# Retention in chunks of 64 tokens on quarters of the PE array, with a second copy of the values

## The chip, the cores and the metric

The program runs on one core of a Trainium2 chip. Its engines are TensorE (PE in the profile, with its weight loads shown as PEld), VectorE (DVE), ScalarE (ACT), GpSimd (POOL) and SyncE (SP), which here issues most DMAs. Each engine works through a fixed list of instructions in order and waits at semaphores for the others. The metric is device time in microseconds for one execution, the median of several runs.

## The reference

The program is a two-layer trunk on 1024 tokens of width 1024, in float32. Layer 0 has two branches, a state-space branch with a GLU, and retention with 8 heads (keys and queries of 64, values of 128); layer 1 is a convolution module. The change touches only the retention, which the reference computes in chunks of 64 tokens:

```python
CHUNK = 64
def retention(q, k, v):
    q = rope(q, positions) * (RET_DK ** -0.5)
    k = rope(k, positions)
    log_g = jnp.log(1.0 - 2.0 ** (-5.0 - jnp.arange(RET_HEADS)))
    intra = jnp.exp(log_g[:, None, None] * jnp.abs(idx[:, None] - idx[None, :]))
    ...
    scores = jnp.einsum('bnihd,bnjhd->bnhij', qc, kc) * intra
    intra_out = jnp.einsum('bnhij,bnjhe->bnihe', scores, vc)
    k_dec = jnp.exp(log_g[None, :] * (CHUNK - 1 - idx)[:, None])
    kv = jnp.einsum('bnjhd,jh,bnjhe->bnhde', kc, k_dec, vc)
    def state_step(s, kv_n):
        return chunk_decay * s + kv_n, s
    _, s_prev = lax.scan(state_step, zeros, kv)
    cross = jnp.einsum('bnihd,ih,bnhde->bnihe', qc, q_dec, s_prev)
    out = intra_out + cross
    mu = jnp.mean(out, axis=-1); var = jnp.mean((out - mu) ** 2, axis=-1)
    return (out - mu) * lax.rsqrt(var + EPS)
```

## The kernel before

Everything lives in one class. The retention is a stage in the middle of layer 0: `retention` (L926) runs four pairs of heads. The two heads of a pair lie on partitions 0 to 63 and 64 to 127, so that one tile of 128 partitions holds the keys (`krot`) or the queries (`qrot`) of both. `ret_proj` projects keys and queries of a pair (the 512-wide products `mm_k` and `mm_q`, through the helper at L276 to L278) and rotates them. `ret_values` (before pair 0) makes the values of all heads by products and sums into the tiles `v`, with 128 tokens on the partitions and the block of tokens as a free index.

`ret_heads` (L1079) does one pair, in blocks of 128 tokens, that is two of the reference's chunks; a mask sets to zero what a query of the first chunk would take from a key of the second. Its steps, in the names of the profile:

- `ktp`, `kt`: the keys are transposed to tokens on partitions (8 products) and multiplied by a decay (DVE, L1090).
- `kv` (L1107): 14 products, per block and head, each on half of the array (128 tokens deep, 64 wide), into two PSUM banks, one for each half of the sequence (`hf`).
- `S` (L1115, L1117): DVE turns them into the states before each block, one after the other: a copy and 6 steps S[b+1] = g S[b] + kv[b]. These form a chain.
- `sp` (L1124): the scores, 16 products, each on half of the rows; a bank for each head and half. `sc` (L1130): the scores times the mask, 4 instructions of 128x512 on DVE.
- `ro`: for each half of the sequence, first the products of states and queries (L1154, half of the rows each, called cross below), then those of masked scores and values (L1159, the full array, called intra below), into a bank for each head.
- `st`, `mv`, `rs`, `on` (L1168 to L1174): mean and variance of each row on DVE, the square root on ACT (L552), the reciprocal on DVE (L553), the normalised rows on DVE. ACT also casts weights for layer 1 in this stage (`lh` from `lf`, L232, made by `weight_low`), and its list of instructions is in order.
- `rt` (L1182): the normalised rows are transposed back, 8 products for each half of the sequence; they wait for `on`. They are multiplied by the gate `grl` and stored.

All of these products are float32, and the profile counts two instructions for each: 14 products of `kv` are 28 matmul rows. A product with a moving side of 512 columns (`mm_...`, in a faster float32 form) is one row.

The order on each engine is no list in the source: a scheduler places the instructions by priority and by a simulated time for each, `issue_after` and `chained` add constraints, and tile pools add waits for free buffers. So the 512-wide products of the next pair's projections (`mm_q`, `mm_k`) and, in the last two pairs, of the GLU (`mm_glu`) stand between the retention products. PSUM has 8 banks: five for the tag "aux" (all of `kv`, `sp`, `ro`, `rt` and others) and three for `mm`.

## Time and profile before

| what | before |
|---|---|
| median of 3 runs | 1178.66 us (1176.93 to 1179.49) |
| span of the profiled execution, first to last instruction | 1173.9 us |
| PE busy in the span | 1161.3 us |
| DVE, ACT, POOL busy | 910.5, 545.1, 713.5 us |
| the profile's chain of work that ended last | 91% on PE |

The profile gives the span of the profiled execution and no other time for it. The median of the runs lies 4.8 us above that span. In the rows below, a timeline row has the start in us, the duration, the engine, the line, the operation, output and inputs, the shape of the array's part that is used (128*64 is 128 rows by 64 columns), the shape of the moving side and the count; at its end in brackets stands how long the engine was idle before it and who released it. "sp<-qrot,krot 64*128 64x128 f32 x18" is 18 matmul instructions on half of the rows.

### The profile page before, as it was taken

The page shows a single profiled execution, that of the slowest core. Times are in us where ns is not written, and L with a number is a line of the kernel's source. Part 1 is how long each engine was busy: PE and PEld are TensorE (multiplying, and loading weights), DVE is VectorE, ACT ScalarE, POOL GpSimd, SP SyncE. Part 2 cuts the span into 40 slices and gives each one's busy share as a digit, 9 for nine tenths or more (in the row PEclk, how much of TensorE's full clock was granted, in tenths as well). Part 3 has the DMA queues.
Part 4 walks back from the last instruction along what each step waited for, and adds up shares of the span by engine and source line. Part 5 has one row for each costly group of instructions (what it writes and reads, how often), then busy time and mean ns, then how long its engine had stood idle before and what let it go on. Part 6 is the DMA issues. An engine that isn't in the chain of part 4 may idle for free.

```text
span 1173.9 us, 17492 instructions
## 1 busy us (share of the span) xinstructions
PE 1161.3 (99%) x6150; PEld 965.5 (82%) x6150; DVE 910.5 (78%) x1507; ACT 545.1 (46%) x821; POOL 713.5 (61%) x507
## 2 busy tenths in 40 slices
...
GB/s 344 109 178 109 134 270 312 272 269 282 273 307 325 268 228 192 251 190 180 362 313 304 160 220 268 309 232 188 161 158 306 216 182 132 134 176 243 281 247 138
DMA packets 131192, 270.66 MB, mean 231 GB/s; under 512 B 12832, under 2 KB 41760, under 8 KB 130976
## 3 DMA queue, kind: packets, MB, share of 16 engines
...
q10 hardware_dynamic: 1152, 4.19, 0.9%
...
## 4 chain that ended last, share of the span: by engine, by line
PE 91%; DMA 4%; DVE 2%; SPq 1%; ACT 1%; POOL 1%; issue 1%; DVEq 0%; POOLq 0%; ACTq 0%
PE mm_g L277 8%; PE mm_g L278 8%; PE mm_g L276 7%; PE mm_w L278 4%; PE mm_w L277 4%; PE mm_w L276 4%; PE mm_a L278 2%; PE mm_b L277 2%; PE mm_a L276 2%; PE mm_b L278 2%; PE mm_a L277 2%; PE mm_b L276 2%; PE mm_u L278 2%; PE mm_oc L278 2%; PE mm_u L277 2%; PE mm_oc L277 2%
## 5 line engine op out<-in xcount | busy, mean ns | idle before, releaser
L1461 DVE SCALAR_TENSOR_TENSOR cv<-u,convw,cv 128x512 f32<-128x512 f32 x358 | 244.7, 750 | 5.0 <-ACT cv L1447 3.5
L1441 POOL TENSOR_TENSOR tp<-tp,tp 128x512 f32<-128x512 f32 x104 | 138.9, 1338 | 28.7 <-ACT tp L1440 23.4
L278 PE MATMUL mm_g<-xh,wl_g 128*128 128x512 f32 x256 | 100.8, 394 | 0.0
L277 PE MATMUL mm_g<-xl,wh_g 128*128 128x512 f32 x256 | 100.7, 394 | 0.0
L276 PE MATMUL mm_g<-xh,wh_g 128*128 128x512 f32 x256 | 100.5, 393 | 0.0
L1440 ACT ACTIVATE tp<-u,convw 128x512 f32<-128x512 f32 x104 | 69.6, 713 | 9.6 <-POOL tp L1441 9.4
L277 PEld LDWEIGHTS mm_g<-xl,wh_g 128*128 128x128 f32 x256 | 48.1, 188 | 11.2 <-issue 1.6
L278 PEld LDWEIGHTS mm_g<-xh,wl_g 128*128 128x128 f32 x256 | 48.0, 188 | 10.5
L276 PEld LDWEIGHTS mm_g<-xh,wh_g 128*128 128x128 f32 x256 | 48.1, 188 | 9.6
L278 PE MATMUL mm_oc<-zh,wl_woc 128*128 128x512 f32 (+1 forms) x152 | 54.5, 360 | 0.2 <-DMA wl_woc<-lo_woc 0.2
L276 PE MATMUL mm_oc<-zh,wh_woc 128*128 128x512 f32 (+1 forms) x152 | 54.3, 362 | 0.0
L277 PE MATMUL mm_oc<-zl,wh_woc 128*128 128x512 f32 (+1 forms) x152 | 54.0, 357 | 0.0
L276 PE MATMUL mm_glu<-yh,wh_glu 128*128 128x512 f32 x128 | 50.0, 392 | 1.3 <-ACT sg L1250 1.3
L277 PE MATMUL mm_u<-xl,wh_u 128*128 128x512 f32 x128 | 50.1, 391 | 1.0 <-DVE xl L390 0.9
L276 PE MATMUL mm_g<-h1h,wh_cg 128*128 128x512 f32 x128 | 50.3, 393 | 0.0
L276 PE MATMUL mm_a<-h1h,wh_ca 128*128 128x512 f32 x128 | 50.3, 393 | 0.0
L278 PE MATMUL mm_b<-h1h,wl_cb 128*128 128x512 f32 x128 | 50.3, 393 | 0.0
L232 ACT CAST lh<-lf 128x512 fp32r<-128x512 f32 x32 | 19.5, 618 | 65.9 <-DMA lf<-w_c 59.3
L278 PE MATMUL mm_a<-h1h,wl_ca 128*128 128x512 f32 x128 | 50.0, 391 | 0.0
L277 PE MATMUL mm_glu<-yl,wh_glu 128*128 128x512 f32 x128 | 50.0, 392 | 0.0
L278 PE MATMUL mm_g<-h1h,wl_cg 128*128 128x512 f32 x128 | 49.9, 390 | 0.0
L277 PE MATMUL mm_g<-h1l,wh_cg 128*128 128x512 f32 x128 | 49.9, 390 | 0.0
...
## 6 DMA issues: line engine op xcount, KB each, us to landing
...
```

Source lines behind the costliest of these rows:

```text
L232: self.nc.scalar.copy(hi[:], f[:])
L276: nc.tensor.matmul(ps, wh[:, kb, :], xh, start=start, stop=False)
L277: nc.tensor.matmul(ps, wh[:, kb, :], xl, start=False, stop=False)
L278: self.last_mm = nc.tensor.matmul(ps, wl[:, kb, :], xh, start=False, stop=stop)
L1440: nc.scalar.mul(sk[:], u[:, k:k + HALF], cw[:, nb, k:k + 1])
L1441: gp.tensor_tensor(s0[:], s0[:], sk[:], op=ALU.add)
L1461: v.scalar_tensor_tensor(dst[:], *tap, accs_[i][:], op0=ALU.mult, op1=ALU.add)
```

## The change

A block becomes a chunk of 64 tokens, as in the reference.

- All products of a pair run on quarters of the array (64 rows by 64 columns). `kv`: 30 instead of 14, in two banks by the parity of the chunk in its block. `sp`: 32 instead of 16, with 64 moving columns instead of 128, and both heads' scores in one bank, on its lower and upper partitions, instead of a bank each. Cross: 30 instead of 14. Intra: 32 on quarters instead of 16 on the full array.
- 15 states instead of 7: a copy and 14 steps on DVE. The masked scores take 2 DVE instructions instead of 4.
- The mask shrinks from 512 KB to 128 KB and the decay table from 256 KB to 4 KB; nothing of a score is set to zero any more.
- On a quarter, the rows that hold the scores of a head must also hold the values, so a chunk whose values lie in the other half of the partitions needs them moved. `crossed(pair)` makes the tile `vx`, the values of the pair with the two halves of each block exchanged, by 4 DMAs of 128 KB from SBUF to SBUF on SP's queue; it is called for pair 0 behind `ret_values`, and for the next pair behind `ret_heads`. There is one buffer for `vx`. `value(..., own=True)` picks it.

```diff
@@ -941,11 +941,11 @@
...
         nc.sync.dma_start(self.rk[:], A["rope_k"])
-        self.mask = r0.tile([P, NH, P], F32, name="retmask")
+        self.mask = r0.tile([P, 4, 64], F32, name="retmask")
         nc.sync.dma_start(self.mask[:], A["ret_mask"])
-        self.g128 = r0.tile([P, 4], F32, name="g128")
-        nc.sync.dma_start(self.g128[:], A["ret_g128"])
-        self.kdec = r0.tile([P, NH, 64], F32, name="kdec")
+        self.g64 = r0.tile([P, 4], F32, name="g64")
+        nc.sync.dma_start(self.g64[:], A["ret_g64"])
+        self.kdec = r0.tile([P, NH], F32, name="kdec")
         nc.sync.dma_start(self.kdec[:], A["ret_kdec"])
...
@@ -955,6 +955,7 @@
...
                     V = self.ret_values(self.pool("vp", 1, stack=vst))
+                self.crossed(0)
                 self.rp = self.pool("ret", 1, stack=st)
...
@@ -970,6 +971,8 @@
...
             self.ret_heads(pair, *cur, V, turned)
+            if pair < 3:
+                self.crossed(pair + 1)
     def ret_proj(self, pair):
...
@@ -1074,7 +1077,22 @@
...
                     self.y_pass(vp, cb)
-        return lambda p, b, hh: vt[p // 2][b // 4][:, b % 4, (2 * (p % 2) + hh) * P:(2 * (p % 2) + hh + 1) * P]
+        def value(p, c, hh, own=False):
+            d, h, b, i = p // 2, c // 8, c // 2 % 4, p % 2
+            if own and c % 2 != hh:
+                return self.vx[:, c // 2, :]
+            return vt[d][h][:, b, (2 * i + hh) * P:(2 * i + hh + 1) * P]
+        return value
+
+    def crossed(self, pair):
+
+        d, i = pair // 2, pair % 2
+        self.vx = self.r0.tile([P, 8, P], F32, name=f"vx{pair}", tag="vx", bufs=1)
+        for h in range(2):
+            for hh in range(2):
+                to, of = slice(64 * hh, 64 * hh + 64), slice(64 - 64 * hh, 128 - 64 * hh)
+                self.nc.sync.dma_start(self.vx[to, 4 * h:4 * h + 4, :],
+                                       self.vt[d][h][of, :, (2 * i + hh) * P:(2 * i + hh + 1) * P])
     def ret_heads(self, pair, K, Q, qadds, V, turned):
...
@@ -1086,51 +1104,43 @@
...
                 nc.tensor.transpose(ps[:, b * P:(b + 1) * P], K[:, t0:t0 + P], self.ident[:])
-            kd = self.kdec[:, 2 * pair:2 * pair + 2, :].rearrange("p h d -> p (h d)")
-            self.last_kt = v.tensor_tensor(kt[:, 4 * hf:4 * hf + 4, :], ps[:].rearrange("p (b d) -> p b d", b=4),
-                                           kd.unsqueeze(1).broadcast_to([P, 4, P]), op=ALU.mult)
+            kd = self.kdec[:, 2 * pair:2 * pair + 2].unsqueeze(1).unsqueeze(3).broadcast_to([P, 4, 2, 64])
+            self.last_kt = v.tensor_tensor(
+                kt[:, 4 * hf:4 * hf + 4, :].rearrange("p b (h d) -> p b h d", h=2),
+                ps[:].rearrange("p (b h d) -> p b h d", b=4, h=2), kd, op=ALU.mult)
         with self.tc.issue_after(self.last_kt.ins):
...
         turned()
-        S = rp.tile([P, 8, P], F32, name=f"S_{pair}", tag="S", bufs=1)
+        S = rp.tile([P, 15, P], F32, name=f"S_{pair}", tag="S", bufs=1)
+        half = lambda i: slice(64 * i, 64 * i + 64)
         for hf in range(2):
-            ps = self.bank(f"kv{hf}_{pair}")
-            for b4 in range(4):
-                b = 4 * hf + b4
-                if b == 7:
-                    continue
-                for hh in range(2):
-                    r = slice(64 * hh, 64 * hh + 64)
-                    nc.tensor.matmul(ps[r, b4 * P:(b4 + 1) * P], kt[:, b, r], V(pair, b, hh),
-                                     start=True, stop=True)
-            for b4 in range(4):
-                b = 4 * hf + b4
-                if b == 7:
-                    continue
-                kv = ps[:, b4 * P:(b4 + 1) * P]
-                if b == 0:
-                    v.tensor_copy(S[:, 1, :], kv)
+            kvs = [self.bank(f"kv{hf}{par}_{pair}") for par in range(2)]
+            cs = [c for c in range(8 * hf, 8 * hf + 8) if c < 15]
+            col = lambda c: slice(c // 2 % 4 * P, (c // 2 % 4 + 1) * P)
+            self.chained(nc.tensor.matmul(kvs[c % 2][half(hh), col(c)], kt[half(c % 2), c // 2, half(hh)],
+                                          V(pair, c, hh)[half(c % 2)], start=True, stop=True)
+                         for c in cs for hh in range(2))
+            for c in cs:
+                kv = kvs[c % 2][:, col(c)]
+                if c == 0:
+                    v.tensor_copy(S[:, 0, :], kv)
                 else:
-                    v.scalar_tensor_tensor(S[:, b + 1, :], S[:, b, :], self.g128[:, pair:pair + 1], kv,
+                    v.scalar_tensor_tensor(S[:, c, :], S[:, c - 1, :], self.g64[:, pair:pair + 1], kv,
                                            op0=ALU.mult, op1=ALU.add)
         self.masked = [None, None]
-        sc = [rp.tile([P, 8, P], F32, name=f"sc{hh}_{pair}", tag=f"sc{hh}", bufs=1) for hh in range(2)]
+        sc = rp.tile([P, 16, 64], F32, name=f"sc_{pair}", tag="sc", bufs=1)
         for hf in range(2):
-            sps = [self.bank(f"sp{hf}{hh}_{pair}") for hh in range(2)]
-            self.chained(nc.tensor.matmul(sps[hh][:, b4 * P:(b4 + 1) * P],
-                                          K[64 * hh:64 * hh + 64, (4 * hf + b4) * P:(4 * hf + b4 + 1) * P],
-                                          Q[64 * hh:64 * hh + 64, (4 * hf + b4) * P:(4 * hf + b4 + 1) * P],
+            sps = self.bank(f"sp{hf}_{pair}")[:].rearrange("p (c i) -> p c i", c=8)
+            tok = lambda c: slice(c * 64, (c + 1) * 64)
+            self.chained(nc.tensor.matmul(sps[half(hh), c % 8, :], K[half(hh), tok(c)], Q[half(hh), tok(c)],
                                           start=True, stop=True)
-                         for b4 in range(4) for hh in range(2))
-            for hh in range(2):
-                self.masked[hf] = v.tensor_tensor(
-                    sc[hh][:, 4 * hf:4 * hf + 4, :], sps[hh][:].rearrange("p (b i) -> p b i", b=4),
-                    self.mask[:, 2 * pair + hh, :].unsqueeze(1).broadcast_to([P, 4, P]), op=ALU.mult)
-
+                         for c in range(8 * hf, 8 * hf + 8) for hh in range(2))
+            self.masked[hf] = v.tensor_tensor(sc[:, 8 * hf:8 * hf + 8, :], sps,
+                                              self.mask[:, pair, :].unsqueeze(1).broadcast_to([P, 8, 64]), op=ALU.mult)
         if pair == 2:
...
@@ -1146,18 +1156,17 @@
...
             def products():
-                for b4 in range(4):
-                    b = 4 * hf + b4
+                cs = range(8 * hf, 8 * hf + 8)
+                out = lambda c, hh: pss[hh][half(c % 2), c // 2 % 4 * P:(c // 2 % 4 + 1) * P]
+                for c in cs:
                     for hh in range(2):
-                        r = slice(64 * hh, 64 * hh + 64)
-                        if b:
-                            yield nc.tensor.matmul(pss[hh][:, b4 * P:(b4 + 1) * P], Q[r, b * P:(b + 1) * P],
-                                                   S[r, b, :], start=b4 == (hf == 0), stop=False)
-                for hh in range(2):
-                    for b4 in range(4):
-                        b = 4 * hf + b4
-                        yield nc.tensor.matmul(pss[hh][:, b4 * P:(b4 + 1) * P], sc[hh][:, b, :],
-                                               V(pair, b, hh), start=False, stop=b4 == 3)
+                        if c:
+                            yield nc.tensor.matmul(out(c, hh), Q[half(hh), tok(c)], S[half(hh), c - 1, :],
+                                                   start=c in (2, 1, 8, 9), stop=False)
+                for c in cs:
+                    for hh in range(2):
+                        yield nc.tensor.matmul(out(c, hh), sc[half(hh), c, :], V(pair, c, hh, True)[half(hh)],
+                                               start=False, stop=c % 8 > 5)
             last_ro = self.chained(products())
...
@@ -1693,14 +1702,13 @@
...
     gam = 1.0 - 2.0 ** (-5.0 - np.arange(NH, dtype=np.float64))
-    i = np.arange(P, dtype=np.float64)
+    i = np.arange(P, dtype=np.float64) % 64
-    jj, ii = np.meshgrid(i, i, indexing="ij")
-    ok = ~((ii < 64) & (jj >= 64))
-    m = np.where(ok[:, None, :], gam[None, :, None] ** (np.abs(ii - jj) - (ii + 1.0))[:, None, :], 0.0)
-    c["ret_mask"] = m.astype(f)
-    c["ret_kdec"] = np.repeat((gam[None, :] ** (127.0 - i)[:, None])[:, :, None], 64, axis=2).astype(f)
-    c["ret_g128"] = np.repeat((gam ** 128.0).reshape(4, 2).T, 64, axis=0).astype(f)
+    jj, ii = np.meshgrid(i, i[:64], indexing="ij")
+    gh = gam.reshape(4, 2).T.repeat(64, axis=0)
+    c["ret_mask"] = (gh[:, :, None] ** (np.abs(ii - jj) - (ii + 1.0))[:, None, :]).astype(f)
+    c["ret_kdec"] = (gam[None, :] ** (63.0 - i)[:, None]).astype(f)
+    c["ret_g64"] = np.repeat((gam ** 64.0).reshape(4, 2).T, 64, axis=0).astype(f)

```

The scheduler lays the lists out anew. **PE, pair 0, from the last intra products to the first transposes `rt`.** Before (in these rows `mm_q` is the next pair's projection, and 27 of its products stand between the last `ro` and the first `rt`; the first and last three of them are shown in the two pieces):

```order
L1159 MATMUL ro_0_4431<-v_1_3500,sc_0_4349 128x128 x4
L1159 MATMUL ro_1_4432<-v_1_3500,sc_0_4350 128x128 x4
L276 MATMUL mm_q_0_4528<-xh_0_174,wh_q_4169 128x512
L277 MATMUL mm_q_0_4528<-xl_0_175,wh_q_4169 128x512
L278 MATMUL mm_q_0_4528<-xh_0_174,wl_q_4170 128x512
```

```order
L276 MATMUL mm_q_1_4554<-xh_1_178,wh_q_4169 128x512
L277 MATMUL mm_q_1_4554<-xl_1_179,wh_q_4169 128x512
L278 MATMUL mm_q_1_4554<-xh_1_178,wl_q_4170 128x512
L1182 MATMUL rt_1_4485<-ident,on_0_4426 128x128 x4
L1182 MATMUL rt_0_4491<-ident,on_0_4408 128x128 x4
```

With the change the same place on PE reads:

```order
L1168 MATMUL ro_0_4489<-vx_4207,sc_4380 64x128
L1168 MATMUL ro_1_4490<-v_1_3500,sc_4380 64x128
L278 MATMUL mm_q_0_4607<-xh_0_174,wl_q_4170 128x512
L276 MATMUL mm_q_0_4607<-xh_0_184,wh_q_4169 128x512
L1191 MATMUL rt_1_4559<-ident,on_0_4484 128x128 x4
L1191 MATMUL rt_0_4565<-ident,on_0_4466 128x128 x4
L277 MATMUL mm_q_0_4607<-xl_0_185,wh_q_4169 128x512
```

Two 512-wide products are left between the last `ro` and the first `rt`; 27 follow between the first and the second group of `rt`. Between the two groups of `sp` of this pair there are now 11 of them instead of 9. The same count in the other pairs, before and now, is 27 and 25 (pair 1), 42 and 38 (pair 2), 37 and 24 (pair 3).

**DVE, pair 0, the states and the masked scores.** Before, from the first state on (`kv_0_4326` and `kv_0_4339` are the two banks):

```order
L1115 COPY S_4325<-kv_0_4326 128x128
L1117 SCALAR_TENSOR_TENSOR S_4325<-S_4325,g_3507,kv_0_4326 128x128 x3
L1117 SCALAR_TENSOR_TENSOR S_4325<-S_4325,g_3507,kv_0_4339 128x128 x2
L1130 TENSOR_TENSOR sc_0_4349<-sp_0_4351,retmask 128x512
L1117 SCALAR_TENSOR_TENSOR S_4325<-S_4325,g_3507,kv_0_4339 128x128
L1130 TENSOR_TENSOR sc_0_4350<-sp_0_4352,retmask 128x512
L1130 TENSOR_TENSOR sc_0_4349<-sp_0_4363,retmask 128x512
L1130 TENSOR_TENSOR sc_0_4350<-sp_0_4364,retmask 128x512
```

With the change, the end of that stretch, after a copy and seven steps:

```order
L1131 SCALAR_TENSOR_TENSOR S_4330<-S_4330,g_3507,kv_0_4357 128x128
L1142 TENSOR_TENSOR sc_4380<-sp_0_4381,retmask 128x512
L1131 SCALAR_TENSOR_TENSOR S_4330<-S_4330,g_3507,kv_0_4358 128x128
L1131 SCALAR_TENSOR_TENSOR S_4330<-S_4330,g_3507,kv_0_4357 128x128
L1131 SCALAR_TENSOR_TENSOR S_4330<-S_4330,g_3507,kv_0_4358 128x128
L1131 SCALAR_TENSOR_TENSOR S_4330<-S_4330,g_3507,kv_0_4357 128x128
L1131 SCALAR_TENSOR_TENSOR S_4330<-S_4330,g_3507,kv_0_4358 128x128
L1131 SCALAR_TENSOR_TENSOR S_4330<-S_4330,g_3507,kv_0_4357 128x128
L1142 TENSOR_TENSOR sc_4380<-sp_0_4399,retmask 128x512
```

The first product of masks stands behind the ninth state, the second behind all 15.

**SP, ahead of pair 0.** SP's list now has the second two transfers of pair 0's `vx` (the first two stand some 20 rows earlier) between two weight loads for layer 1 (`lf`) and the loads of the gates (`grl`) and of a later pair's weights (`wf_q`):

```order
L231 DMA lf_4218<-w_c 128x512
L231 DMA lf_4225<-w_c 128x512
L1094 DMA vx_4207<-v_1_3500 64x4x128 x2
L1152 DMA grl_4417<-gr_d 128x1024
L1152 DMA grl_4419<-gr_d 128x1024
L1152 DMA grl_4870<-gr_d 128x1024
L265 DMA wf_q_5053<-w_ab 128x1024
```

Before, `grl` stood right behind the two `lf`. The transfers of `vx` wait for the last sum of the values on DVE. On ACT the list is the same in both kernels at this place: six casts `lh` of layer 1's weights stand ahead of the first square root `rs` of pair 0.

## The prediction

> **What bounds the kernel now.** I read the page's totals and its chain first, then the list of waits of PE within the retention stage (430 to 620 us), then the timelines of PE, DVE and ACT in pair 0, the pair whose order changes most.
>
> ```profile
> span 1173.9 us, 17492 instructions
> PE 1161.3 (99%) x6150; PEld 965.5 (82%) x6150; DVE 910.5 (78%) x1507; ACT 545.1 (46%) x821; POOL 713.5 (61%) x507
> PE mm_glu L276 <- ACT sg L1250: 1.3, 1, 1.3
> PE rt L1182 <- DVE on L1174: 1.0, 1, 1.0
> PE kv L1107 <- DVE kt L1090: 0.7, 1, 0.7
> PE rt L1182 <- DVE mv L1169: 0.3, 1, 0.3
> ```
>
> PE is busy for 99% of the span and waits 3.3 us in all in this stage. So PE time saved shortens the program, and a new wait of PE lengthens it. DVE, at 78%, has room on average only; what matters is what PE waits for at a given place.
>
> ```profile
> 447.49 1.75 PE L1107 MATMUL kv<-v,kt 128*64 128x128 f32 x28
> ...
> 450.48 0.51 PE L276 MATMUL mm_q<-xh,wh_q 128*128 128x512 f32 x1
> ...
> 452.77 1.04 PE L1124 MATMUL sp<-qrot,krot 64*128 64x128 f32 x13
> ...
> 456.51 1.16 PE L1154 MATMUL ro<-S,qrot 64*128 64x128 f32 x16
> 457.60 2.05 PE L1159 MATMUL ro<-v,sc 128*128 128x128 f32 x16
> 459.41 0.48 PE L276 MATMUL mm_q<-xh,wh_q 128*128 128x512 f32 x1
> ...
> 465.42 0.39 PE L278 MATMUL mm_q<-xh,wl_q 128*128 128x512 f32 x1
> 466.07 1.06 PE L1182 MATMUL rt<-ident,on 128*128 128x128 f32 x8 [0.27 <-DVE mv L1169]
> ```
>
> Matmuls overlap, so I count from start to start. The retention products of pair 0 take 450.48 - 447.49 = 2.99 us and 459.41 - 452.77 = 6.64 us, 9.63 us in all. A full-array product takes (459.41 - 457.60)/16 = 0.113 us, a half-array one about half of that: 16 of the cross products would be 0.91 us by it and take 457.60 - 456.51 = 1.09. I put the missing 0.2 us down to the switch between array shapes. The 27 `mm_q` rows from 459.41 to 465.42 take 0.231 us each.
>
> **PE's products.** The trace has products on quarters of the array in another stage:
>
> ```profile
> 108.80 0.45 PE L882 MATMUL kp<-Mr,s_s_cbr 128*32 128x128 f32 x8
> 109.04 0.42 PE L883 MATMUL kp<-Mi,s_s_cbi 128*32 128x128 f32 x8
> ```
>
> Eight start within 0.24 us, 0.030 us each, about a quarter of 0.113; I take 0.028. The change issues 2 x (30 + 32 + 30 + 32) = 248 rows for each pair: 248 x 0.028 = 6.94 us, and with three switches 7.5 us against 9.6. That is **-2.1 us a pair, -8.4 us in all**. These quarters are 128 rows by 32 columns, not 64 by 64. Were 64x64 tiles to run only two at a time, the 184 rows other than `sp` would cost 0.056 each, 5.2 us more a pair, and the term would be +12; that is the far end, and I take the near row because both halves by rows and halves by columns run side by side in this trace.
>
> The scores are the weakest of the four. Only two of the four quarters are used in turn, so 0.028 us needs a row of 64 moving columns to take half of one of 128. The nearest rows say that it may not:
>
> ```profile
> L547 PE MATMUL ss<-ones,ssum x16: 223/275/276, 34.8 to 36.4; 128*128 128x64 f32 x16
> L1159 PEld LDWEIGHTS ro<-v,sc 128*128 128x128 f32 x128 | 14.9, 192 | 1.0
> L1107 PEld LDWEIGHTS kv<-v,kt 128*64 128x64 f32 x112 | 6.0, 137 | 2.0 <-DVE kt L1090 0.9 <-issue 0.7 <-DVE qrot L1003 0.4
> ```
>
> Sixteen products with 64 moving columns take (36.4 - 34.8)/15 = 0.107 us, as long as with 128. But they load 128 columns of weights each, and the load gets shorter with the columns (192 ns against 137 for 64), so I hold the load for what limits them, and the scores load 64. If the 0.107 holds for them all the same, 64 scores at 0.053 cost 3.4 us instead of 1.8: +1.6 us a pair. I take nothing and keep that as a rival.
>
> A rule speaks for that dearer price by another way. Before, the two heads' scores, on different rows, went to two banks; with the change they share one. The Trainium skill, "TensorEngine Tiling (Array Packing)", section "Gotcha 1: PSUM Pressure", says that different row tiles cannot access the same PSUM bank simultaneously. By it the two quarters would take turns and the sum would rise by the same 1.6 to 1.8 us a pair; no row of before has two row tiles in one bank, so the trace neither bears it out nor speaks against it.
>
> **Pair 0: a new wait.** Before, 27 `mm_q` stood between the last `ro` and the first `rt` and covered the chain from `ro` to `on`. Now there are 2. The chain does not come sooner:
>
> ```profile
> 448.96 1.95 DVE L1117 SCALAR_TENSOR_TENSOR S<-S,g,kv 128x128 f32<-128x128 f32 x5
> 450.82 0.68 DVE L1130 TENSOR_TENSOR sc<-sp,retmask 128x512 f32<-128x512 f32 x1
> ...
> 457.58 0.30 DVE L1169 BATCH_NORM_AGGREGATE mv<-st 128x2 f32<-128x6 f32 x3
> ...
> 462.43 1.37 DVE L1174 TENSOR_SCALAR on<-ro,mv,rs 128x128 f32<-128x128 f32 x4
> ...
> 464.57 1.36 DVE L1174 TENSOR_SCALAR on<-ro,mv,rs 128x128 f32<-128x128 f32 x4
> 459.95 0.62 ACT L232 CAST lh<-lf 128x512 fp32r<-128x512 f32 x1 [6.53 <-POOL krot L1000]
> 460.59 1.28 ACT L552 ACT_TABLE_LOAD   x1
> 461.88 0.30 ACT L552 ACTIVATE rs<-mv,reteps 128x4 f32<-128x4 f32 x1
> 453.55 0.38 SPq L231 DMA_DIRECT2D lf<-w_c  x1
> ```
>
> DVE has the statistics at 457.9. ACT is not ready to take the square root: it idles 6.53 us before the cast `lh`, loads a table, and gives `rs` at 462.2. The releaser named is POOL, but the cast reads `lf`, and that transfer was issued at 453.55 only, so I take the transfer for what ended last; either way it does not hang on PE's products. The same six casts stand ahead of `rs` in the changed list. Then DVE makes the eight `on` of the first half, 462.4 to 465.9, with 0.8 us of other statistics between them (463.80 to 464.57) that move away: `on` would be ready at about **465.2**.
>
> PE, from 447.49 on: `kv` 1.7 and `sp` 0.9 to 450.1, a switch, 11 `mm_q` (2.5) to 452.8, a switch, `sp`, cross, intra, cross and intra at 0.8 to 0.9 each with 0.2 of switch to 457.4, a switch and 2 `mm_q`: 458.1. DVE's 14 steps at 0.39 and two masks at 0.6 end at about 455.7 and hold none of these. The first `rt` would wait 465.2 - 458.1 = 7.1 us where it waited 0.27: **+6.8 us**. If ACT were free the wait would be 457.9 + 1.3 + 0.3 + 2.9 - 458.1 = 4.3; if transfers of `vx`, earlier on the same queue, push `lf` back by one of its neighbours' durations, it would be some 2 us longer.
>
> **The clock.** The trace shows PE idle at both ends:
>
> ```profile
> 1.05 4.96 PE L366 MATMUL idle<-ones 128*128 128x128 f32 x28 [1.05 <-DVE epst L311]
> 1167.05 0.70 PE L562 MATMUL rf_R<-rf_dg,ones 128*128 128x256 f32 x2
> 1170.00:1172.00 2.00, 0.00 (x0) 0.93 1.09 380
> 1172.00:1174.00 2.00, 0.00 (x0) 0.50 0.17 57
> ```
>
> After the last product ends at 1167.75, the granted clock (the column behind the busy time) is 0.50 from about 1171.7: it halves after some 4.0 us of idling. A wait of 7.1 us crosses that. At the start, 28 products took 4.96 us instead of 28 x 0.113 = 3.2, so the way back costs 1.8; I take **+2.0 us**, between 0 (wait below 4 us) and 3.2. The Trainium skill, "TensorE: Matmul & The Clock Gate", section "Part 1: The HAM clock gate (the "warmup" mystery)", puts the idle window at about 3.4 us and free-running; the trace's 4.0 agrees, and by it a wait of 4 us might already be dear.
>
> **Pairs 1, 2 and 3.** In pair 1 `on` is there long before `rt`:
>
> ```profile
> 500.14 1.35 DVE L1174 TENSOR_SCALAR on<-ro,mv,rs 128x128 f32<-128x128 f32 x4
> 505.67 1.03 PE L1182 MATMUL rt<-ident,on 128*128 128x128 f32 x8
> 529.55 5.74 DVE L1194 TENSOR_TENSOR yl<-yf,yh 128x512 fp32r<-128x512 f32 x4
> 544.83 1.06 PE L1182 MATMUL rt<-ident,on 128*128 128x128 f32 x8 [1.04 <-DVE on L1174]
> ```
>
> 4.2 us of room (505.67 - 501.49); PE comes 2.1 + 2 x 0.23 = 2.5 sooner: no wait, **0**. Pair 2 had a wait of 1.04. PE comes 2.1 + 4 x 0.23 = 3.0 sooner, and DVE has 8 x 0.39 - 2 x 0.6 = 1.9 more to do; in full, the wait would grow by 4.9. Against it, the four `yl` took 1.4 us each, with waits for loads in them, and PE is by then about 4 us later against the loads (+8.8 - 4.2), so they cost DVE less; at best the old wait goes too, -1.0. I take **+1.0**.
>
> ```profile
> 562.70 0.69 DVE L1251 SCALAR_TENSOR_TENSOR sg<-sg,yg 128x512 f32<-128x512 f32 x1 [1.49 <-POOL yg L1246]
> 563.73 1.04 PE L1124 MATMUL sp<-qrot,krot 64*128 64x128 f32 x13
> 565.03 0.73 DVE L1117 SCALAR_TENSOR_TENSOR S<-S,g,kv 128x128 f32<-128x128 f32 x2
> ```
>
> In pair 3 the states are scattered between other work of DVE, and the sixth step ended at 565.76, behind `sg`, which waits for POOL. Before, the first cross product needs one state and can start at once; now it stands later in a longer chain. PE would have the second `sp` done near 563.1 (six fewer `mm_glu`, 1.4 us), so cross would wait up to 2.7, and the seven steps of the second half another 0.9. The waits of 0.7 and 1.3 of before may go in return, and the loads come relatively sooner: between -2.0 and +3.6; I take **+1.5**.
>
> **Free edits.** DVE's +1.9 us a pair outside these places lies beside PE. The smaller tables save 640 KB of loads long before they are needed. The 16 transfers of `vx` take time on SP's list and the DMA engines:
>
> ```profile
> 431.61 5.63 DVE L1044 SCALAR_TENSOR_TENSOR v<-mm_v,Rtok,v 128x512 f32<-128x512 f32 x8 [2.57 <-PE mm_v L1064]
> ```
>
> Those of pair 0 wait for the last of these sums at 437.2, 17 us ahead of intra; queued behind them on SP are `grl` and `wf_q`, for which PE and DVE have no use until the end of this pair. Those of the later pairs have a whole pair's time. I take 0, at worst 1 us a pair if weight loads behind them come late.
>
> **Sum.** -8.4 + 6.8 + 2.0 + 1.0 + 1.5 = +2.9 us on the profiled span of 1173.9, or 1176.8; the median of the runs lies 4.8 above that span: **1181.6 us**. About 2.4 us (0.2%) is what a measurement can tell from no change.
>
> **Rivals.**
> - *The first wait is short* (0.22): ACT gets `lf` early, the wait is 4.3 or less and the clock stays up: -8.4 + 4.0 + 0 + 1.0 + 1.5 = -1.9, **1176.8**, at or just below the bound of faster. It decides at a wait of 4 us. Against it is ACT's idle time of 6.53 us before that cast.
> - *No waits of note* (0.08): the other way, all on one mechanism: DVE and ACT are ahead of PE everywhere. -8.4: **1170**. Against it is 457.9 for the statistics themselves.
> - *Scores at the old rate* (0.12): the two quarters take turns, by the short moving side or by the shared bank. +1.6 a pair, swallowed by the wait in pair 0, +4.8 elsewhere: **1186.4**. All quarters two at a time, a small part of this chance, would reach 1197. (The rule of the Trainium skill on PSUM banks, above, would give this case.)
> - *Late transfers* (0.10): `vx` ahead of weight loads on SP's list, `lf` 2 us later and a second drop of the clock: +5, **1186 to 1188**.
>
> **Chances.** Forecast 0.48 (1179 to 1185). Range 1174 to 1190: it leaves out most of the second rival and the far end of the third. Faster (below 1176.3): the second rival, half of the first: 0.19. Same: the rest of the first and the low edge of the forecast: 0.27. Slower: 0.54.
>
> **What would show it.** Rows of 64*64 at 0.028 us from start to start, `sp` of a half within 0.9 us (1.7 for the third rival); the first `rt` of pair 0 idle for about 7 us behind `on`, with a granted clock of 0.5 right after it; no wait in pair 1; in pair 3 a `ro` that waits for `S`. I am wrong if `rs` of pair 0 runs much before 460, or if the retention products of a pair take 9 us or more.

## The result and the profile after

| | before | after |
|---|---|---|
| median of the runs | 1178.97 us (1176.93 to 1179.49) | **1191.94 us** (1190.52 to 1192.71) |
| ratio, 95% interval | 1 | 1.0116 (1.0101 to 1.0130) |
| span of the profiled execution | 1173.9 us | 1188.7 us |

The changed kernel is 13.0 us slower by the medians, 1.2% by the ratio. The two profiled executions differ by more, 14.8 us in their spans. First the head of its page, then its waits of PE over the whole span (engine, tile and line, releaser, us in total, times, longest):

```profile
span 1188.7 us, 18562 instructions
PE 1160.4 (98%) x6662; PEld 964.2 (81%) x6662; DVE 916.4 (77%) x1531; ACT 542.8 (46%) x819; POOL 712.4 (60%) x507
```

```profile
PE rt L1191 <- DVE on L1183: 8.1, 2, 7.3
PE rt L1191 <- DVE mv L1178: 3.7, 1, 3.7
PE ro L1164 <- DVE S L1131: 2.3, 2, 2.1
PE mm_w L278 <- DVE wl_p L167: 2.2, 1, 2.2
PE ro L1164 <- issue: 1.9, 1, 1.9
```

PE is busy for almost as long as before, but waits for some 15 us more. The busy time hides a gain, since PE counts as busy at half its clock too. Its timeline shows where:

```profile
448.08 1.85 PE L1123 MATMUL kv<-v,kt 64*64 64x128 f32 x58
...
449.88 1.09 PE L1139 MATMUL sp<-qrot,krot 64*64 64x64 f32 x30
450.90 0.50 PE L276 MATMUL mm_q<-xh,wh_q 128*128 128x512 f32 x1
...
466.22 1.94 PE L1191 MATMUL rt<-ident,on 128*128 128x128 f32 x8 [7.28 <-DVE on L1183]
...
468.38 0.63 PE L278 MATMUL mm_q<-xh,wl_q 128*128 128x512 f32 x1
...
538.77 0.27 PE L1164 MATMUL ro<-S,qrot 64*64 64x128 f32 x1 [1.91 <-issue]
...
552.61 1.19 PE L1191 MATMUL rt<-ident,on 128*128 128x128 f32 x8 [3.74 <-DVE mv L1178]
...
574.67 1.36 PE L1164 MATMUL ro<-S,qrot 64*64 64x128 f32 x27 [2.08 <-DVE S L1131]
...
661.86 0.50 PE L278 MATMUL mm_w<-ysh,wl_p 128*128 128x512 f32 x1 [2.22 <-DVE wl_p L167]
```

The products do what was forecast: 58 rows of `kv` start within 449.68 - 448.08 = 1.60 us, 0.028 us each, and `kv` with the first half's scores is done in 2.82 us. Behind the waits a 512-wide product takes 0.63 us instead of 0.39. The view by windows (start and end, length, busy time of PE, PEld, DVE, ACT and POOL with the number of instructions, granted clock, DMA share, GB/s) has the clock there:

```profile
461.25:471.49 10.24, 5.27 (x17) 4.53 (x18) 8.41 (x37) 3.47 (x8) 6.08 (x5) 0.50 0.47 118
553.41:556.82 3.41, 3.41 (x11) 2.73 (x10) 3.37 (x10) 0.88 (x3) 1.65 (x1) 0.50 0.63 138
662.64:666.05 3.41, 3.41 (x9) 2.63 (x8) 3.41 (x7) 0.00 (x0) 0.00 (x0) 0.50 0.86 285
```

PE worked for 5.27, 3.41 and 3.41 us at 0.50, which at full clock is half of that: 2.6 + 1.7 + 1.7 = 6.0 us lost.

Pair 0 on ACT and DVE:

```profile
460.75 0.62 ACT L232 CAST lh<-lf 128x512 fp32r<-128x512 f32 x1 [4.27 <-DMA lf<-w_c]
...
462.68 0.48 ACT L552 ACTIVATE rs<-mv,reteps 128x4 f32<-128x4 f32 x2
...
540.86 1.27 ACT L1201 CAST yh<-yf 128x512 fp32r<-128x512 f32 x2 [4.90 <-DMA yf<-yn_d]
```

```profile
458.12 0.49 DVE L1178 BATCH_NORM_AGGREGATE mv<-st 128x2 f32<-128x6 f32 x6
...
464.70 1.36 DVE L1183 TENSOR_SCALAR on<-ro,mv,rs 128x128 f32<-128x128 f32 x4
```

The statistics are there at 458.6. ACT casts a late `lf`, loads the table for the square root and gives `rs` at 462.68 and after, and `on` ends at 466.06. PE starts `rt` 0.16 us later. The last ACT row belongs to pair 2, whose first `kv` was at 527.73: the fifth cast of `yf` (to `yh`) in its first part comes 540.86 - 527.73 = 13.13 us behind it. Before, the same cast and DVE's work on the pair read:

```profile
531.48 1.28 ACT L1192 CAST yh<-yf 128x512 fp32r<-128x512 f32 x2 [5.76 <-DMA yf<-yn_d]
```

```profile
522.08 1.75 PE L1107 MATMUL kv<-v,kt 128*64 128x128 f32 x28
```

That is 531.48 - 522.08 = 9.40 us. The load for this cast stands in SP's list behind a store of `lh`. After:

```profile
524.91 0.32 SPq L236 DMA_DIRECT2D lo_cb<-lh  x1
...
533.31 1.01 SPq L1232 DMA_DIRECT2D yf<-yn_d  x2
```

SP waits 5.0 us for POOL's `lh` ahead of this store. The store is issued 2.8 us ahead of the first `kv` and the load 5.6 us behind it; before, the store was issued 7.1 us ahead and the load 1.5 us behind. DVE in pair 2 after:

```profile
528.86 0.29 DVE L1129 COPY S<-kv 128x128 f32<-128x128 f32 x1 [3.29 <-PE kv L1123]
...
536.12 2.49 DVE L1203 TENSOR_TENSOR yl<-yf,yh 128x512 fp32r<-128x512 f32 x4
541.51 2.46 DVE L1203 TENSOR_TENSOR yl<-yf,yh 128x512 fp32r<-128x512 f32 x2 [2.91 <-ACT yh L1201]
543.90 1.67 DVE L1177 BATCH_NORM_STATS2 st<-ro 128x6 f32<-128x128 f32 x8
545.50 1.43 DVE L1203 TENSOR_TENSOR yl<-yf,yh 128x512 fp32r<-128x512 f32 x1
...
547.14 0.65 DVE L1203 TENSOR_TENSOR yl<-yf,yh 128x512 fp32r<-128x512 f32 x1
...
551.12 1.35 DVE L1183 TENSOR_SCALAR on<-ro,mv,rs 128x128 f32<-128x128 f32 x4
```

and before:

```profile
523.22 0.29 DVE L1115 COPY S<-kv 128x128 f32<-128x128 f32 x1 [4.69 <-PE kv L1107]
...
536.01 0.98 DVE L1194 TENSOR_TENSOR yl<-yf,yh 128x512 fp32r<-128x512 f32 x1
...
538.90 0.65 DVE L1194 TENSOR_TENSOR yl<-yf,yh 128x512 fp32r<-128x512 f32 x1
...
542.07 2.61 DVE L1174 TENSOR_SCALAR on<-ro,mv,rs 128x128 f32<-128x128 f32 x8
```

From the first state to the last `on` DVE took 544.68 - 523.22 = 21.46 us and now takes 552.47 - 528.86 = 23.61, 2.15 more. The eight `yl` took 5.74 + 2 x 0.98 + 2 x 0.65 = 9.0 and now take 2.49 + 2.46 + 1.43 + 0.65 = 7.0, 2.0 less. In return DVE idles 2.91 us for the fifth `yh`, where it idled 0.80 for `sp`, and has its 1.9 us of more states. PE comes only 0.6 us sooner, since it stood still for 1.9 us between two products (the row "issue"). So `rt` waits 2.7 us more.

### The profile page after: what moved, and what is told of

Same layout as the page of the kernel before. It is cut to its first block, busy times and chain, and to the rows that moved or that the text cites. A ratio compares the mean times of both kernels' runs of the same rounds, so it can differ in the third digit from the quotient of the medians.

```text
span 1188.7 us, 18562 instructions
## 1 busy us (share of the span) xinstructions
PE 1160.4 (98%) x6662; PEld 964.2 (81%) x6662; DVE 916.4 (77%) x1531; ACT 542.8 (46%) x819; POOL 712.4 (60%) x507
## 4 chain that ended last, share of the span: by engine, by line
PE 82%; DMA 7%; DVE 4%; issue 3%; POOL 1%; ACT 1%; SPq 1%; DVEq 0%; POOLq 0%; ACTq 0%
PE mm_g L277 7%; PE mm_g L278 7%; PE mm_g L276 7%; PE mm_w L278 4%; PE mm_w L276 4%; PE mm_w L277 4%; DMA lf<-w_c 3%; PE mm_a L278 2%; PE mm_a L276 2%; PE mm_b L277 2%; PE mm_a L277 2%; PE mm_b L278 2%; PE mm_b L276 2%; PE mm_u L278 2%; PE mm_oc L278 2%
## 5 line engine op out<-in xcount | busy, mean ns | idle before, releaser
L1255 POOL TENSOR_TENSOR yg<-yg,yn 128x512 f32<-128x512 f32 x16 | 23.7, 1484 | 49.0 <-DMA yg<-gs_d 27.4
L278 PE MATMUL mm_glu<-yh,wl_glu 128*128 128x512 f32 x128 | 50.7, 396 | 0.0
```

The source lines that it names most:

```text
L278: self.last_mm = nc.tensor.matmul(ps, wl[:, kb, :], xh, start=False, stop=stop)
L1255: gp.tensor_tensor(yg[:], yg[:], yn[:], op=ALU.mult)
```

## The experiments

All are edits of the changed kernel. Stages are read on PE: a pair from its first `kv` to the next pair's; "pair 3, GLU" from the first `kv` of pair 3 to the first `mm_w` (the output projection); then its first 96 products; then the rest. Medians and ratios are of several runs. The kernel before was timed again beside each group of them (medians of 1176.69 to 1178.97 us), so small differences are read from the ratios. Stage lengths come from one profiled execution each, and pair 2 scatters between 35.4 and 38.6 us among kernels whose engines do the same work there in the same order (after, e4, e6, e8, e12, e14).

| run | median us | ratio to before (95%) | pair 0 | pair 1 | pair 2 | pair 3, GLU | 96 mm_w | rest |
|---|---|---|---|---|---|---|---|---|
| before | 1178.97 | 1 | 40.01 | 34.57 | 31.87 | 89.33 | 21.76 | 502.33 |
| after | 1191.94 | 1.0116 (1.0101-1.0130) | 47.30 | 32.34 | 35.44 | 90.33 | 25.99 | 502.78 |
| e1 | 1187.81 | 1.0082 (1.0067-1.0097) | 38.37 | 34.71 | 38.90 | 90.30 | 25.45 | 502.24 |
| e2 | 1198.40 | 1.0166 (1.0149-1.0183) | 40.45 | 32.34 | 45.15 | 95.26 | 26.21 | 502.43 |
| e4 | 1192.40 | 1.0121 (1.0106-1.0136) | 47.75 | 32.34 | 38.60 | 90.69 | 24.53 | 503.66 |
| e5 | 1198.91 | 1.0178 (1.0160-1.0195) | 47.25 | 32.34 | 38.10 | 95.71 | 25.65 | 502.78 |
| e6 | 1192.02 | 1.0122 (1.0101-1.0143) | 47.01 | 32.34 | 35.75 | 90.90 | 25.56 | 502.92 |
| e7 | 1193.06 | 1.0132 (1.0111-1.0152) | 38.26 | 35.22 | 37.16 | 96.14 | 24.29 | 503.75 |
| e8 | 1189.90 | 1.0103 (1.0078-1.0127) | 48.33 | 32.34 | 35.94 | 91.11 | 25.15 | 504.49 |
| e10 | 1186.57 | 1.0074 (1.0050-1.0098) | 42.12 | 32.34 | 35.15 | 90.35 | 28.11 | 505.66 |
| e11 | 1182.55 | 1.0036 (1.0021-1.0052) | 37.33 | 32.34 | 36.02 | 89.97 | 27.14 | 502.80 |
| e12 | 1188.06 | 1.0078 (1.0050-1.0106) | 43.34 | 32.34 | 36.79 | 90.69 | 24.81 | 504.98 |
| e13 | 1196.27 | 1.0172 (1.0149-1.0194) | 46.76 | 32.34 | 35.31 | 93.50 | 25.91 | 502.07 |
| e14 | 1189.00 | 1.0103 (1.0086-1.0121) | 47.21 | 32.34 | 38.34 | 90.41 | 23.11 | 502.01 |
| e15 | 1189.04 | 1.0107 (1.0090-1.0124) | 47.16 | 32.34 | 34.52 | 90.07 | 25.37 | 502.25 |
| e16 | 1181.39 | 1.0032 (1.0021-1.0044) | 38.45 | 32.42 | 34.48 | 91.10 | 25.94 | 502.15 |
| e17 | 1192.24 | 1.0111 (1.0090-1.0131) | 47.88 | 32.34 | 30.28 | 95.40 | 27.89 | 502.27 |
| e18 | 1195.81 | 1.0137 (1.0113-1.0161) | 47.47 | 32.34 | 34.73 | 93.88 | 27.17 | 502.25 |
| e19 | 1194.89 | 1.0138 (1.0111-1.0166) | 44.67 | 37.39 | 36.11 | 94.51 | 23.35 | 502.75 |
| e20 | 1180.77 | 1.0020 (1.0006-1.0034) | 38.15 | 32.57 | 34.45 | 90.49 | 21.93 | 504.78 |

The expectations name theories by letters. In short: D, `vx` on SP's list is in the way; E and H, the `yl` stand ahead of the statistics on DVE; F, subtractions for `lh` on DVE hold the output projection; G, the loads of pair 2 are late, behind the chain of `lf`, `lh` and its store; H', in the output projection `wl_p` stands behind `yr0g` on DVE; J, two bounds act together in pair 2; K, DVE's work in all bounds the stretch of pair 2 to the GLU. Any other letter is the theory that the text beside it describes.

### Pair 0: e1, e2, e4, e12

e1 makes the products of `mm_q` of pair 1 stand between the last `ro` and the first `rt` of pair 0 again:

```diff
-            self.ret_heads(pair, *cur, V, turned)
+            heads = self.ret_heads(pair, *cur, V, turned)
+            next(heads)
+            if pair in (0,):
+                nxt = list(ahead)[-1]
+                self.behind = self.last_mm
+            list(heads)
```

> Only the place of the first transposes rt of pair 0 is changed: they stand behind the last product of the next pair's projection, 37 mm_q behind the last ro instead of 2. The changed kernel waits 7.3 us there and then runs 5.3 us at half clock: 7.0 us of new wait and 2.6 us of clock. Theory A (that loss is one of its own, the waits in pair 2 and before the output projection have other causes): rt of pair 0 waits under 1 us, no half clock near 461, the time falls by 9 to 10 us from 1192 to about 1182, the later waits stay within 2 us of what they were. Theory B (the later waits follow from PE being 8 us late): they shrink too, 1174 to 1178. Theory C (the loads do not move along with PE, so that PE only meets them earlier): pair 2's waits grow by what pair 0 saves, 1186 or more.

Pair 0 gets 8.9 us shorter, a little below what it took before. So the wait and the low clock behind it are the loss there, all but some 0.6 us (40.01 - 2.2 = 37.8, against 38.37). But pair 1 gets 2.4 and pair 2 3.5 us longer, and the kernel gains only 4.1 us, as theory C expects. The 3.5 us alone would be little more than pair 2's scatter; that about half of the gain comes back as loss later is what the median shows. Its waits of PE in pair 2 and the GLU:

```profile
PE rt L1201 <- DVE mv L1185: 4.0, 1, 4.0
PE mm_glu L277 <- DVE yl L1213: 3.0, 3, 2.0
```

e2 takes the casts of `lf` out of pair 0 and deals all 18 to pairs 1 and 2:

```diff
-                for k in range(LOWS * pair // 3, LOWS * (pair + 1) // 3) if pair < 3 else ():
+                for k in range(LOWS * (pair - 1) // 2, LOWS * pair // 2) if pair in (1, 2) else ():
```

> The six casts lh of layer 1's weights that stand ahead of pair 0's square root on ACT are moved to pairs 1 and 2 (nine each instead of six); all else as in the changed kernel. Theory A (rs of pair 0 is late because ACT, in order, waits for the transfer lf): rs comes right after the statistics and a table load, at about 459.5 instead of 462.7, on ends near 462.5, the first rt waits about 4 us instead of 7.3, and the clock is at half for at most one stretch of 3.4 us: 4 to 6 us less, unless the nine loads in pairs 1 and 2 cost some of it back. Rival (rs waits for something else on ACT or DVE): rs stays within 1 us of 462.7 and the time within 2 us of 1192.

Pair 0 takes 40.45 us and PE's wait in it is 3.0 us: ACT's list is indeed what made most of the wait there. With nine casts in pair 2 that pair takes 45.15 us, and the kernel is slower in all.

e4 issues `vx` on ACT's queue, and e12 leaves `vx` out, so that some products read the wrong half of the values and the result is not the retention's:

```diff
-                self.nc.sync.dma_start(self.vx[to, 4 * h:4 * h + 4, :],
+                self.nc.scalar.dma_start(self.vx[to, 4 * h:4 * h + 4, :],
```

> The 16 transfers of vx are issued from ACT's list instead of SP's; the order of PE is that of the changed kernel but for one mm_q. Theory D (on SP's list they wait for the intra products and hold the loads behind them, which makes yf, yh and yl of pair 2 and the loads of the output projection late): the first rt of pair 2 waits under 2 us instead of 3.7, the wait of 2.2 us and the half clock in the output projection go, 1184 to 1188. Rival (the loads are late for their own order and their own waits): both waits within 1 us of what they were, the time within 2 us of 1192.

```diff
-                self.crossed(0)
...
-            if own and c % 2 != hh:
-                return self.vx[:, c // 2, :]
```

> The changed kernel without the second copy of the values: the 16 transfers vx are left out, and the intra-chunk products whose chunk and head differ in parity read the other half's values, so that the retention's result is another one; products, waits on other engines and all else are the same. If the transfers (2 MB, and their places on SP) are what makes the loads late: pair 2 shrinks by 2 us or more, and the whole by 3 to 6 us. Theory G with SP's order of lo, lf and yf as the cause: within 2 us of the changed kernel.

e4 changes nothing in the whole that can be measured. Without the transfers pair 0 is 4.0 us shorter (43.34), which is all of e12's gain of 3.9 us; pair 2 is no shorter, so D does not explain it. ACT's row in e12 shows why pair 0 is shorter:

```profile
459.17 0.56 ACT L552 ACTIVATE rs<-mv,reteps 128x4 f32<-128x4 f32 x2 [8.03 <-DVE mv L1173]
```

The scheduler has put the six casts far ahead, at 370 to 403 us, so that the square root now waits for the statistics alone, and PE's wait is 3.0 us as in e2. That is a gain of order on ACT and not shown to be a price of the transfers; it shows once more what the wait in pair 0 hangs on.

### Pair 2: e5 to e8, e10, e11

e5 puts the last four `yl` behind `on`; e6 gives the low halves of `lh` to POOL; e7 is e1, e5 and e6 together; e8 puts three loads of `yf` behind loads of `lf` on SP's list:

```diff
-                self.split(f, a, b, v, None if halves else self.masked_2 if h == 0 else ...
+                self.split(f, a, b, v, None if halves else (self.masked_2 if kb < 4 else self.on_2) if h == 0 else ...
```

> As the changed kernel, but in pair 2 the last four of the eight subtractions yl (of the GLU's first operand) are held behind the normalised rows on of the first half; six of the eight stood ahead of the first statistics st, and they wait for the transfers yf. Theory E (pair 2's wait for on is DVE held, in order, by yl that wait for loads): st of the first half starts within 2 us of its last ro instead of 8, the first rt of pair 2 waits under 1 us instead of 3.7 and the half clock near 553 goes, some 4 us less up to there; mm_glu may wait up to 2 us for yl in return: 1186 to 1190. Rival (the chain on DVE is too long in any order): the wait only moves to mm_glu or to the second rt, within 2 us of 1192.

```diff
-                self.weight_low(lp, k, (("cs", "pilot"), ("cq", "sq")), 1)
+                self.weight_low(lp, k, (("cs", "pilot"), ("cq", "sq")), 1, gp)
```

> As the changed kernel, but behind the retention the subtractions lh of layer 1's weights run on POOL instead of DVE. Theory F (in the stage before the output projection DVE, in order, is held by an lh whose transfer lf is late; what follows on DVE, ACT and the loads yr0f then comes 2 to 3 us later against PE): the wait of mm_w for wl_p (2.2 us) and the half clock behind it go, 3 to 4 us less behind the GLU, 1188 to 1189. Rival (the loads themselves are late): the wait stays within 1 us, the time within 1.5 us of 1192.

> The changed kernel with three moves together: rt of pair 0 behind 37 mm_q, the last four yl of pair 2 behind on, the subtractions lh behind the retention on POOL. If the losses are three (pair 0: 9.6 us, pair 2: 4 to 6, output projection: 4) and each is met where it arises: 1192 - 18 = 1174, faster than before by the 8 us that the quarters save less some new waits, 1172 to 1178. Rival (what is saved in one place is waited for in the next, since DVE and the loads of pair 2 bound the stage): above 1181.

```diff
+                        after = {0: 13, 2: 15, 3: 15}.get(kb) if h == 0 else None
+                        with self.tc.issue_after(self.lfs[after].ins) if after else nullcontext():
+                            nc.sync.dma_start(f, src[rows(kb), hs(h)])
```

> The changed kernel with one edit: on SP the third and fourth y load (yf 2 and 3 of the first half) stand behind the weight load lf 15, where they stood ahead of lo/lf 14 and 15, as they did not before. Theory G (SP's in-order list sets when the loads of pair 2 arrive, and with them pair 2's length): the fifth cast yh comes 9.5 to 11 us after the first kv of pair 2 instead of 13.1, pair 2 takes 32 to 33.5 us instead of 35.4, and the whole is 2 to 3.5 us below the changed kernel. Rival (pair 2 is set by DVE's own order, yl ahead of the statistics): pair 2 stays at 35 to 36 us and the whole within 1.5 us of the changed kernel.

e5 is 7 us slower: `rt` still waits, 15.3 us in three places (7.6 of them in pair 0), since the square roots stand behind casts `yh` on ACT that wait for their own loads; the GLU then waits for the late `yl`. In e6 the wait for `wl_p` is still 2.2 us and the 96 products take 25.56 us, so F falls. e8 leaves pair 2 where it was (35.94), but it does not test G: the fifth `yh` came 13.0 us behind the first `kv` there too, so the edit did not bring the load forward. e7 gains in pair 0 what e1 gained, and loses it in pairs 1 and 2 and the GLU.

e10 casts 13 weight halves here instead of 18 (the other five are made later), and e11 is e10 with e1:

```diff
-LOWS = 18
+LOWS = 13
```

> The changed kernel with 13 instead of 18 of the 32 weight halves (lf, lh, lo) made in the retention stage (4, 4, 5 in pairs 0, 1, 2), the other five in the GLU part behind it. Theory G: two fewer rounds of load, cast, subtraction and store ahead of the y loads of pair 2: the fifth yh at most 11 us after the first kv of pair 2, pair 2 31.5 to 33.5 us long, and pair 0 at least 2 us shorter since two casts fewer stand ahead of the square root on ACT; what the five cost in the GLU part is unknown, 0 to 5 us. Rival: pair 2 as before, 35 to 36 us.

> The same with the first experiment's edit as well (transposes of pair 0 behind all the products of the next q projection). Theory G: pair 0 38 to 39 us, pair 2 32 to 34 us instead of the 38.9 of that experiment, so about 5 us below it, 1180 to 1184 us in all. Rival (what is saved is always waited for at the next place): 1186 to 1189 us.

Pair 0 is 5.2 us shorter, since two fewer casts stand ahead of the square root, and PE's wait there is 3.0 us; the output projection pays 2.1 and the rest 2.9. The fifth `yh` comes 11.7 us behind the first `kv` and pair 2 takes 35.15, both short of what G expects. With e1 the kernel takes 1182.55: pair 0 and pair 1 are now better than before, pair 2 is not.

### Pair 2: one bound or two: e13, e15, e17, e18

e13 puts the first four pairs of statistics ahead of all `yl`, which removes H. e15 deals the 13 casts 6, 7 and 0 to the pairs, which removes G:

```diff
-                self.split(f, a, b, v, None if halves else self.masked_2 if h == 0 else ...
+                self.split(f, a, b, v, None if halves else self.mv_2 if h == 0 else ...
```

> The changed kernel with one edit: in pair 2 the subtractions yl of the first half (DVE) stand behind the statistics mv of the first half of this pair, not ahead of them; loads and SP's order as they are. Theory H (the wait of pair 2 is one of order on DVE: six yl, and with them the wait for the loads yf, stand ahead of the statistics): the first rt of pair 2 waits less than 1 us instead of 3.7, no low clock there, pair 2 30 to 32 us instead of 35.4, and the whole 3 to 5 us below the changed kernel. Rival (the loads bound this pair however DVE is ordered): the wait comes back at the glu products, which need yl, and the stretch from the first kv of pair 2 to the end of the glu part shrinks by less than 1.5 us.

```diff
-                for k in range(LOWS * pair // 3, LOWS * (pair + 1) // 3) if pair < 3 else ():
+                for k in range((0, 6, 13, 13)[pair], (0, 6, 13, 13)[pair + 1]) if pair < 3 else ():
```

> The changed kernel with the weight halves dealt 6, 7, 0 to pairs 0, 1, 2 (before 6, 6, 6) and the other 19 in the glu part: ahead of the y loads of pair 2 no lf, lh, lo is left, so nothing on SP waits for ACT and POOL there. Theory G (pair 2 ends by its loads, and these stand behind the chain lf, lh, lo): the fifth yh at most 9 us after the first kv of pair 2 (13.1), pair 2 30 to 32.5 us (35.4, single looks up to 38), no low clock in it; pair 1 up to 2 us longer by its seventh. Against the run with 4, 4, 5 the whole 2 to 4 us less, 1182.5 to 1184.5. Rival (the y loads are held by the traffic of kswp, grl and yr as well, or by DVE): pair 2 stays above 34.5 us.

> The changed kernel with both edits of pair 2 that did nothing alone: weight halves dealt 6, 7, 0 (loads early), and the first half's yl behind the first half's statistics on DVE. Theory J (two bounds of nearly the same length in pair 2, the loads and DVE's order; each hides the other): pair 2 30 to 32 us with the first rt waiting less than 1 us and glu less than 2, no low clock, the whole 3 to 5 us below the run with the dealing alone, 1184 to 1186. Rival (a third thing, such as the slots of the loads that yl frees, is next): pair 2 above 34 us, or the gain gone at the glu products.

> The same, but the first four yl stay ahead of the statistics and only the later ones stand behind, so that the slots of the loads come free 4 us earlier. Theory J: the first rt waits up to 2 us, pair 2 31 to 33 us, glu without a wait on yh; the whole within 1.5 us of the run above. Rival of the slots: here the glu products do not wait and the whole is 2 us or more below the run above.

e17 is both edits; e18 is both with only the last four `yl` behind the statistics. Waits of PE in this stage, e13:

```profile
PE rt L1193 <- DVE on L1185: 8.8, 2, 7.8
PE mm_glu L276 <- ACT yh L1203: 4.6, 2, 2.5
PE mm_glu L277 <- DVE yl L1205: 1.3, 1, 1.3
```

The wait for `on` in pair 2 is gone (the 7.8 is pair 0's), but `mm_glu` waits 5.9 us for `yh` and `yl`, 3.9 of them in pair 2, and pair 2 is as long as without the edit. The stretch to the GLU's end gets 3.0 us longer, and so H alone falls. In e15 the loads are early, and the wait stays, as these rows of PE's waits, of ACT and of DVE show:

```profile
PE rt L1191 <- DVE mv L1178: 3.8, 1, 3.8
```

```profile
532.75 1.29 ACT L1201 CAST yh<-yf 128x512 fp32r<-128x512 f32 x2 [6.82 <-DMA yf<-yn_d]
```

```profile
536.09 5.53 DVE L1203 TENSOR_TENSOR yl<-yf,yh 128x512 fp32r<-128x512 f32 x6
541.55 1.67 DVE L1177 BATCH_NORM_STATS2 st<-ro 128x6 f32<-128x128 f32 x8
```

DVE does not idle for the fifth `yh` any more (the ACT row; it stands 5.1 us behind the first `kv`); it goes through six `yl` on end and reaches the statistics at about the same time. G alone falls too. With both gone, e17's pair 2 takes 30.28 us, 1.6 less than before the change and 5.2 less than after it, and its waits are:

```profile
PE rt L1193 <- DVE on L1185: 7.8, 1, 7.8
PE mm_glu L276 <- ACT yh L1203: 3.1, 2, 1.9
PE ro L1168 <- DVE sc L1142: 2.9, 1, 2.9
```

Of the waits of `rt` only pair 0's is left, and `mm_glu` waits 1.2 us in pair 2. So J holds for the wait in pair 2: either cause alone is enough to keep it. Its forecast for the whole (1184 to 1186) failed, for the time comes back later: pair 2 and the stretch to the GLU's end together take 125.7 us in e17 and 125.8 after the change (121.2 before), and the kernel takes 1192.24. e18 gains nothing by the middle way (128.6).

### The output projection and the sums: e14, e16, e19, e20

e14 puts DVE's four `yr0g`, two of which wait for loads, behind the `wl_p` that PE waits for:

```diff
-                        v.tensor_tensor(f[:], f[:], t2f[kb][:], op=ALU.subtract)
+                        with self.tc.issue_after(self.wl_of["p1_1"].ins):
+                            v.tensor_tensor(f[:], f[:], t2f[kb][:], op=ALU.subtract)
```

> The changed kernel with one edit in the output projection: DVE's low part wl_p of the second weight stands ahead of the four subtractions yr0g - t2f, which wait for transfers. Theory H' (this wait too is one of order on DVE): mm_w waits less than 0.7 us instead of 2.2, no low clock there, the first 96 mm_w 22 to 23 us instead of 26.0, and the whole 3 to 4.3 us below the changed kernel. Rival (ACT's cast or the transfers are next at the same place): the first 96 mm_w stay above 25 us.

The order on DVE that it changes is this one, of the changed kernel, and e14's row of PE's waits follows:

```profile
656.05 0.69 DVE L1325 TENSOR_TENSOR yr0g<-yr0g,t2f 128x512 f32<-128x512 f32 x1 [0.64 <-DMA yr0g<-yr_d]
...
659.35 1.32 DVE L1325 TENSOR_TENSOR yr0g<-yr0g,t2f 128x512 f32<-128x512 f32 x2 [1.41 <-DMA yr0g<-yr_d]
660.59 1.22 DVE L167 TENSOR_TENSOR wl_p<-wf_p,wh_p 128x1024 fp32r<-128x1024 f32 x1
```

```profile
PE mm_w L280 <- DVE wl_p L168: 1.1, 1, 1.1
```

The wait for this weight is gone, one of 1.1 us for the next comes in its place (the last row, of e14), no low clock follows, and the 96 products take 2.9 us less. So H' holds for this wait, a little short of its figures. What the kernel gains by it is not shown: the ratio of 1.0103 lies inside the interval of the changed kernel. PE also came later to this place, since pair 2 was 2.9 us longer, and e4, e6, e8, e12 and e15, which lack the edit, have no low clock here either and take 24.5 to 25.6 us.

e16 joins what helped: e1, e15's dealing, and `yr0g` with the operands next to it behind the third `wl_p`. e19 tries all 18 casts in pairs 0 and 1 (9, 9, 0), with e1, e14 and e18's order. e20 is e16 with `yr0g` behind the fourth `wl_p`, and the last four `yl` of pair 2's first part on POOL, behind the square roots:

```diff
-                self.split(f, a, b, v, ...
+                self.split(f, a, b, gp if not halves and h == 0 and kb >= 4 else v, ...
+                           self.rs_2 if not halves and h == 0 and kb >= 4 else None)
```

> The same dealing, with the transposes of pair 0 behind the whole next q projection, and in the output projection wl_p of the second and third weight ahead of yr0g - t2f and of the casts t2. If each of the three waits is a wait of its own: pair 0 37 to 38.5 us, pair 2 30 to 32.5, the first 96 mm_w 22 to 23.5, and the whole 1171 to 1176 us, below the kernel before by 0.2 to 0.6 per cent. Rival (what is saved is waited for at the next place): 1178 us or more.

> A candidate for the fastest: the weight halves dealt 9, 9, 0, all 18 ahead of the glu part as in the changed kernel, the transposes of pair 0 behind the whole next q projection, the later yl of pair 2 behind the statistics, wl_p of the second weight ahead of yr0g - t2f. If the waits are separate and each edit takes its own away: pair 0 37 to 39 us, pair 1 32.3 to 34, pair 2 31 to 33, the first 96 mm_w 22 to 23.5, the whole 1168 to 1174, below the kernel before. Rival (lateness moves on): 1178 or more.

> The changed kernel with: transposes of pair 0 behind the whole next q projection; weight halves dealt 6, 7, 0; in pair 2 the last four yl of the first half on POOL instead of DVE (POOL stands idle for 11 us there) and their casts yh, but for one, behind the first half's square roots on ACT; in the output projection the casts and subtractions of t2 and yr0g behind wl_p of the fourth weight. Theory K (from the first kv of pair 2 to the end of the glu part DVE's own work is the bound, so work taken off DVE comes out, while work only reordered comes back): from the first kv of pair 2 to the first mm_w 119 to 122.5 us (125.6 in the run without the move to POOL), and the whole 1174 to 1179. Rival (the loads bound that stretch): 124.5 us or more there, and 1180 or more in all.

e16 takes 1181.39 us; its 96 products take 25.94, since a wait for `wl_p` of 3.5 us is back at the fourth weight. e19 keeps pair 0 at 44.67 and pays in pair 1 and the GLU; it takes 1194.89. e20 is the best that I found, 1180.77 us over twelve runs, 11.2 of the 13.0 us regained; its ratio of 1.0020 (1.0006 to 1.0034) is still not below the kernel before. It has the stretch from the first `kv` to the first `mm_w` back (195.66 us against 195.79 before and 205.41 after) and the output projection too (21.93 against 21.76). It loses the rest: 2.5 us later on, where a wait of 1.2 us for the weight halves that were left for later shows (second row), and a wait for `on` of 5.4 us in pair 2:

```profile
PE rt L1205 <- DVE on L1194: 6.9, 3, 5.4
PE mm_a L280 <- DMA wl_ca<-lo_ca: 1.2, 1, 1.2
```

Its four `yl` on DVE stand beside a rotation on POOL, and take 5.97 us instead of the 2.49 above. K asked for a gain in the stretch of pair 2 to the GLU; at 34.45 + 90.49 = 124.9 us there is hardly one, and the rival's figures hold. But DVE was hardly relieved ahead of the statistics (six `yl` took 6.41 us there in e16), so K is not settled by this run.

## Why the prediction was right and wrong

The forecast was +2.9 us (1181.6), the range up to 1190, and slower the likeliest sign. The sign held; the size was off by 10 us. By its terms, as the two traces show them:

| term | forecast | measured | from |
|---|---|---|---|
| products | -8.4 | -7.7 | pair 1, which has no wait: 32.34 - 34.57 = -2.2, and as much in pairs 0 and 2; pair 3 -1.0, since its stage got 1.0 longer with 2.0 more of waits |
| first wait, pair 0 | +6.8 | +7.0 | 7.28 - 0.27 |
| clock | +2.0 | +6.0 | the three windows at 0.50 |
| pair 2 | +1.0 | +4.6 | `rt` 3.74 - 1.04, and the stop of 1.9 |
| pair 3 | +1.5 | +1.5 | its waits of 2.3, 0.8, 0.2 and 0.2, less 1.3 and 0.7 before |
| no term | 0 | +2.2 | `mm_w` waits for `wl_p` |
| sum | +2.9 | +13.6 | the spans differ by 14.8 |

Of the 1.2 us that are left, 0.6 come before the first `kv` and 0.4 behind the 96 products. The medians differ by 13.0 only. Two steps failed, the clock and pair 2, and one place was left out.

**Products.** The rows run at 0.028 us on 64 by 64 quarters, and the scores do not keep their old rate: 30 of them span 1.0 us. The third rival falls, and with it, for this kernel, what the Trainium skill says in "TensorEngine Tiling (Array Packing)", section "Gotcha 1: PSUM Pressure": the two heads' scores on different row tiles now share a bank, and no cost of it shows (26 rows of the second half start within 0.77 us, 0.030 each). The forecast took the same saving in all four pairs; in pair 3, where the products of states and queries wait for `S` and then start more slowly, it was half of that.

**Pair 0.** The mechanism held: `rs` at 462.68 (462.2 forecast), `rt` idle for 7.28 us (7.1). PE and `on` both came 0.8 to 0.9 us later than forecast, 0.6 of it because the pair began later, so the wait kept its size. That it hangs on ACT's list is shown by e2, that with its clock it is nearly the pair's whole loss by e1. "The same six casts stand ahead of `rs`" was right; e2, e10 and e12, with ACT free in time, have a wait of 3.0, where the forecast put 4.3 for that case. The first rival (the wait is short) falls. So does the fourth (late transfers of `vx`): in e4, with `vx` off SP's list, the last cast ahead of `rs` stands at 460.9, against 460.7. A second and a third drop of the clock came in another way.

**The clock.** The first failed step is "I take **+2.0 us**, between 0 (wait below 4 us) and 3.2": 6.0 were lost. The term was mis-sized twice. It took one stretch from the idle end of the program and let it cost 1.8 to 2.0 us; the stretch behind the first wait lasted to 5.3 us after it and cost 2.6. And it took 4.0 us of idling as the point: the waits of 3.74 and 2.22 us, both shorter, were followed by low stretches too, 1.7 us each.

**Pair 2.** The second failed step is this: "Against it, the four `yl` took 1.4 us each, with waits for loads in them, and PE is by then about 4 us later against the loads (+8.8 - 4.2), so they cost DVE less". The loads have no fixed time. They stand in SP's list behind stores that wait for `lh`, so a late `lh` makes them late too, and the fifth `yh` came 13.1 us behind the first `kv` where it had come 9.4. e15 shows that link: with no `lf` in pair 2 it comes at 5.1. Nor were there waits in the 1.4 us: DVE ran beside POOL. The `yl` did get cheaper, by 2.0 us, and DVE lost it to idling for the load; with the states' 1.9 us the wait grew. That two bounds act at once is shown by e13, e15 and e17.

**No term.** The forecast ended its walk at pair 3. In the output projection DVE's list now has four `yr0g` ahead of the `wl_p` of the second weight, where it had one, and two of them wait for loads. e14 shows that this order makes the wait of 2.2 us. With its clock that is 3.9 of the 4.2 us by which the 96 products got longer, and e20, which puts `yr0g` behind four weights, has them back (21.93). Why the lists came out in this order is not shown. It was one more place where a list in order hands a delay on.

**Open.** The 1.9 us stop of PE in pair 2 at 536.9 has no releaser in the trace. Instructions were being fetched in that stretch (one packet of that queue) while the DMA engines were at 98 to 111% of their share, and the change has 1070 more instructions; that the fetch made PE stop is inferred, and no run tried it. It occurred once at this length (e10 shows 0.5 us). It hardly matters for the time: e4, e6, e8, e12 and e14, with the same order of work in pair 2, have no such stop, and PE waits there for 5.5 to 6.7 us in all, against 5.65; their `mm_glu` wait 1.2 to 2.9 us for `yl` in its place. Nor did a run move POOL's work away, so what DVE's running beside POOL costs the kernel in all stays open, and no version was found that beats the kernel before.
